# Norms issued a stage ahead of their transposes in a hybrid decoder layer, last sums stored from ScalarE's queue, the second block's operands loaded ahead

## The chip, the cores and the metric

The kernel runs on one core of one Trainium2 chip. The core has TensorE (PE; its weight loads are shown apart as PEld), VectorE (DVE), ScalarE (ACT), GpSimd (POOL) and SyncE (SP, which here only issues DMAs). The metric is the device time of one execution in microseconds (us), lower is better. A profile is one execution seen by the hardware profiler; its span runs from the first to the last recorded instruction.

## What is computed

One layer of a hybrid decoder on 2048 tokens of width 1024, in float32:

```python
h = rmsnorm(x, g_mix); z = h @ w_in
y_a = rwkv7_mix(...) @ w_out_a;  y_b = multiscale_pool_mix(...) @ w_out_b
merged = gates[:, :, 0] * y_a + gates[:, :, 1] * y_b
x = x + merged @ w_o
h = rmsnorm(x, g_mlp)
x = x + jnp.square(jax.nn.relu(h @ w_ff1)) @ w_ff2          # 1024 -> 4096 -> 1024
h = rmsnorm(x, g_ple)
x = x + jax.nn.sigmoid(h @ w_ple_gate) * (p @ w_ple_proj)   # gate stage
return rmsnorm(x, g_final)
```

The change touches the end of `merged @ w_o`, the MLP and the gate stage.

## The kernel before

**Matrix products.** A float32 operand is split into two parts of a type that PE takes at full rate (`split`, L1101 to 1103): ACT casts the value (L1102), DVE or POOL subtracts the cast from it (L1103). A product of two split operands is three matmuls (`mm3`, through L133). Transposes are PE instructions too (`tr`, L137).

**Order.** PE executes in the order of the program. A scheduler orders the instructions of the other engines and of SP's DMA queue by its own timeline; on the chip each engine and each queue then runs strictly in that order, waiting where it has to.

**Norm.** `norm_tile` (L173) norms 128 tokens: ACT squares and sums the row (L160, tile `junk`), DVE makes the reciprocal root of it in ten small steps (L165, L149 to 155) and multiplies the tile (L173, 128x1024).

**Stage B of the token mixer** ends with `merged @ w_o`, `stage_B(NB - 1, None)`, a generator that hands over control some 87 times. Between its steps the heads of the MLP's block 0 run (`heads0`, `head`, L1105 to 1162): for each of four token groups j, load and norm two tiles of the stage's result, 16 transposes in two halves, and the sums and differences of the quarters (`A11`, `S1`, ...) for a product scheme with 7 instead of 8 block products. In `head` norm and transposes of one group follow one another, and one step is made at every third hand-over from n = 34. Behind the loop `combine` (L1167 on) loads and prepares the first weights of the MLP.

**MLP layer 1** runs 16 pairs of hidden slices for each of two blocks of 1024 tokens (`pair`), 7 products of 12 matmuls each, and stores the activations to memory. During block 0, from pair 2, two steps of `heads1` per pair make block 1's operands, again norm and transposes in a row, and store them to `hD`. In the last pair of block 0, `load_home` fetches each operand of block 1 once its slot has been used last.

**MLP layer 2** has 56 products (2 blocks, 4 chunks, 7 products), each 48 matmuls on four pairs of operand tiles. The tiles come from a ring: 6 of the pool `hx` and 12 of `f3`. For each pair ACT casts both, POOL subtracts for the one and DVE for the other, and POOL forms the weights' sums. In the last chunk of each block DVE adds up the results and SP stores them to `x2D` (L1393): 16 stores a block.

**Gate stage**, 16 tiles j of 128 tokens: `norm_in` (load from `x2D`, norm, 8 transposes into `rc`, split into `ht`), `embed` (tile of p, 2 transposes, split), `gate(j, n)` for the two halves n of the columns (24 matmuls each), `put(j, n)` (6 matmuls with `wp` into `rp`, tanh on ACT, DVE products, final norm and store). In iteration j of the loop the norm and transposes of tile j+3 and the embedding of j+1 come ahead of gate j; the buffers for `xt` are two. The gate weights `wg` come in four loads of two rows of k each, both column halves together.

## Time and profile before

| what | us |
|---|---|
| median of 3 runs | 3462.11 (3458.47 to 3463.95) |
| the profiled execution: its own time | 3463.73 |
| its span, first to last instruction | 3461.9 |
| token mixer, to the last product of `merged @ w_o` | about 0 to 1721 |
| MLP layer 1 | 1721.75 to about 2434 |
| MLP layer 2 | about 2434 to 3055 |
| gate stage | 3055 to 3461.9 |
| granted clock of PE, mean over the span | 0.949 |

How to read the rows that follow: an engine's timeline gives start, duration, engine, line, operation and tiles (out <- in), how many instructions the row sums up, and in brackets how long the engine was idle ahead of it and what ended that. The granted clock is the share of its full rate that PE was allowed; after idle time it is below 1.00 for a while.

### The profile page before, as it was taken

Reading aid. Unit: us, or ns where it says so; the run is one execution under the profiler, and the core shown is the slowest. Engines: PE = TensorE matmul, PEld = TensorE weight load, DVE = VectorE, ACT = ScalarE, POOL = GpSimd, SP = SyncE. Lnnn points to the kernel's source line nnn. Section 1 sums busy time; section 2 is a strip of 40 time slices with the busy share of each in tenths; the row PEclk is TensorE's granted clock in tenths of the full one; section 3 lists DMA queues with packets and bytes.
Section 4 is the critical chain, followed back from the end, with each engine's and each line's share of the span. In section 5 each row is a group of like instructions: output and inputs, shape, how many; then the busy total and the mean of one; then the engine's idle time right before and its main releaser. Section 6 shows DMA issues by size and latency. Waiting matters only on the chain. (4 is left out here: it accounts for less than half of the span.)

```text
span 3461.9 us, 44299 instructions
## 1 busy us (share of the span) xinstructions
PE 3093.9 (89%) x14409; PEld 2515.9 (73%) x14409; DVE 2473.3 (71%) x5424; ACT 1336.5 (39%) x2774; POOL 1669.3 (48%) x1657
## 2 busy tenths in 40 slices
PE   7999999999999988798788898999899999957678
PEld 6777777777878777676576676888788878845556
DVE  4489888888888889852776867766676976764444
ACT  4446544554455444321322223222444354421111
POOL 4655444434334445311254547565998898820000
PEclk9999999999999999899898999999999999978888
DMA  7866767666666667677444555444644645341211
GB/s 242 248 212 209 237 196 235 226 225 193 209 215 206 196 220 255 210 274 260 151 161 150 180 178 199 144 152 147 246 147 145 216 161 183 110 165 66 72 61 50
DMA packets 421923, 636.41 MB, mean 184 GB/s; under 512 B 174206, under 2 KB 286396, under 8 KB 390460
## 3 DMA queue, kind: packets, MB, share of 16 engines
q1 hardware_dynamic: 421692, 633.59, 55.4%
q8 instruction: 114, 1.87, 0.2%
q14 instruction: 117, 0.96, 0.1%
HBM read 439.49 MB, written 193.99 MB: 183 GB/s over the span
## 5 line engine op out<-in xcount | busy, mean ns | idle before, releaser
L133 PE MATMUL d<-big,wf 128*128 128x512 f32 (+1 forms) x3288 | 849.1, 406 | 14.6 <-DVE wf L244 7.0
L133 PEld LDWEIGHTS d<-big,wf 128*128 128x128 f32 x3288 | 610.2, 193 | 152.6 <-DVE wf L244 9.3
L1103 DVE TENSOR_TENSOR op<-w,op 128x512 fp32r<-128x512 f32 x224 | 300.6, 1361 | 129.6 <-ACT op L1102 127.6
L1103 POOL TENSOR_TENSOR op<-hr,op 128x512 fp32r<-128x512 f32 x224 | 340.3, 1537 | 68.0 <-ACT op L1102 67.9
L133 PE MATMUL d<-op 128*128 128x512 f32 x1344 | 313.9, 392 | 8.9 <-ACT op L1102 5.1
L133 PEld LDWEIGHTS d<-op 128*128 128x128 f32 x1344 | 253.0, 189 | 65.3 <-ACT op L1102 5.5
L1102 ACT CAST op<-hr 128x512 fp32r<-128x512 f32 x224 | 139.1, 621 | 308.9 <-PE rc L133 91.0
L872 DVE TENSOR_TENSOR Xtmp<-Xt,At 128x16 f32<-128x16 f32 (+15 forms) x512 | 243.0, 475 | 9.3
L1103 POOL TENSOR_TENSOR op<-wr,op 128x512 fp32r<-128x512 f32 x96 | 139.3, 1460 | 212.5 <-ACT op L1102 212.5
L133 PE MATMUL d<-yx,wf 128*128 128x512 f32 x768 | 208.5, 418 | 21.2 <-ACT yx L390 13.8
L133 PE MATMUL d<-wf,big 128*128 128x512 f32 x768 | 202.3, 417 | 25.6 <-DVE t2k L611 17.3
L133 PE MATMUL d<-wg,ht 128*128 128x512 f32 x768 | 199.1, 417 | 0.0
L133 PEld LDWEIGHTS d<-wf,big 128*128 128x128 f32 x768 | 148.2, 198 | 64.2 <-DVE t2k L611 20.5
L1250 POOL TENSOR_TENSOR t<-t,t 128x512 f32<-128x512 f32 x128 | 188.8, 1485 | 10.9 <-issue 5.6
L133 PEld LDWEIGHTS d<-yx,wf 128*128 128x128 f32 x768 | 148.2, 199 | 58.4 <-ACT yx L390 15.5
L133 PEld LDWEIGHTS d<-wg,ht 128*128 128x128 f32 x768 | 153.9, 203 | 36.8
L1102 ACT CAST op<-wr 128x512 fp32r<-128x512 f32 x192 | 110.2, 618 | 178.8 <-DMA wr<-in_w_ff_dram 111.1
L133 PE MATMUL rp<-op 128*128 128x512 f32 x672 | 172.4, 391 | 2.8 <-POOL op L1103 2.8
L133 PE MATMUL rc<-op 128*128 128x512 f32 x672 | 171.1, 390 | 0.6 <-DVE accP L1384 0.6
L244 POOL TENSOR_TENSOR wf<-wr,wf 128x640 fp32r<-128x640 f32 (+2 forms) x69 | 120.3, 1745 | 76.4 <-ACT wf L241 71.8
L1102 ACT CAST op<-w 128x512 fp32r<-128x512 f32 x224 | 138.1, 617 | 45.6 <-POOL w L1344 20.6
L875 DVE TENSOR_REDUCE Xt<-Xtmp 128x8 f32<-128x16 f32 (+15 forms) x512 | 147.4, 288 | 9.2
(317 smaller groups left out, 6419.4 us busy)
## 6 DMA issues: line engine op xcount, KB each, us to landing
wf<-wc SPq DMA_DIRECT2D x131, 1024.0 KB, 5.3
wc<-wf SPq DMA_DIRECT2D x50, 1024.0 KB, 6.4
wr<-in_w_ff_dram SPq DMA_DIRECT2D x64, 512.0 KB, 4.9
w<-in_w_ff_dram SPq DMA_DIRECT2D x64, 512.0 KB, 6.2
wr<-in_w_in_dram SPq DMA_DIRECT2D x51, 512.0 KB, 4.5
zD<-t2k SPq DMA_DIRECT2D x96, 256.0 KB, 3.9
zs<-zD SPq DMA_DIRECT2D x32, 640.0 KB, 6.3
At<-aD SPq DMA_DIRECT2D x32, 512.0 KB, 5.2
```

What stands on the lines that cost most here:

```text
L133: PE.matmul(out_, lhsT, rhs, start=start, stop=stop, **kw)
L244: eng.tensor_tensor(wf[:, 1, c], raw[:, c], hi.bitcast(F32)[:, c], ALU.subtract)
L872: DVE.tensor_tensor(tmp[:, :, :, 0:n], Xt[:, :, 0:n].unsqueeze(2).broadcast_to([P, MCOL, FS, n]), At[:, 0:n, r:n].rearrange("p s r -> p r ...
L875: DVE.tensor_reduce(Xt[:, :, r:n].unsqueeze(3), tmp[:, :, :, 0:n], AX.X, ALU.add)
L1102: ACT.copy(out=dst[0], in_=src)
L1103: eng.tensor_tensor(dst[1], src, dst[0].bitcast(F32), ALU.subtract)
L1250: eng.tensor_tensor(out_, a, b, op)
```

## The change

Six edits:

1. `head` is cut in two: `normed` (load and norm) and `head` (transposes and sums). `heads0` norms two groups ahead, at hand-overs 2 and 12; transposes follow at every fourth hand-over from 33, and `combine` is called at n = 86, inside the loop.
2. `heads1` spreads a group over three pairs: norm, first eight transposes, second eight; it starts at pair 1.
3. `load_home` only loads, `fill_home` splits; the first two loads are issued ahead of the last pair of block 0, each fill issues the load after the next.
4. The ring of MLP layer 2 has 10 instead of 12 tiles of `f3` (16 in all). The norm vector and the norms of gate tiles 0 and 1 are issued four products before the end, their transposes inside the last product; the operand tiles of `hx` hold the result.
5. The 16 stores of the last block's sums go to ACT's DMA queue.
6. The gate weights come by column halves, 4 rows of k a load. In the loop, the load and norm of tile j+3 and the transposes of tile j+2 stand behind the first half of gate j, the embedding of j+1 behind the second; `xt` has three buffers.

```diff
+        def normed(blk, j, pool, xt, junk):
             for e, x_ in enumerate(xt):
                 SP.dma_start(out=x_, in_=x1D[...])
                 norm_tile(pool, x_, gb, x_, junk)
-                yield
+            return xt
+        def head(blk, j, xt, tmp, pss):
...
         def heads0():
+            xts = [norm0(0)]
+            yield
+            xts.append(norm0(1))
+            yield
             for j in range(4):
-                yield from head(0, j, fg, load, t2k, dict(tag="t2k", bufs=5), (rps, cps))
+                hd = head(0, j, xts.pop(0), t2k, (rps, cps))
+                next(hd)
+                yield
+                next(hd)
+                yield
+                next(hd, None)
+                if j + 2 < 4:
+                    xts.append(norm0(j + 2))
+                yield
+        steps = {2, 12, *range(33, 33 + 4 * 12, 4)}
         for n, y in enumerate(stage_B(NB - 1, None)):
-            if n >= 34 and n % 3 == 0:
+            if n in steps:
                 next(hg, None)
-        for _ in hg:
-            pass
-        ops_next = combine(fg, 0, WR, t2k)
+            if n == 86:
+                ops_next = combine(fg, 0, WR, t2k)
...
+    def fill_home(nm):
+        raw = hraws.pop(nm)
         for k, eng in ((slice(0, 2), DVE), (slice(2, 4), POOL)):
             split(...)
+        n = USE.index(nm) + 2
+        if n < len(USE):
+            load_home(USE[n])
...
     def heads1():
         for j in range(4):
-            yield from head(1, j, f2, load, tmp2, dict(tag="t2", bufs=NT2), (dps, dps))
+            xt = normed(1, j, f2, [t[:, 0, :], t[:, 1, :]], dict(tag="t2", bufs=NT2))
+            yield
+            hd = head(1, j, xt, tmp2, (dps, dps))
+            next(hd)
+            yield
+            for _ in hd:
+                pass
+            yield
...
+        if blk + 1 < NBLK and pr == NPR - 1:
+            for nm in USE[0:2]:
+                load_home(nm)
-        if blk == 0 and pr >= 2:
-            next(hg, None)
+        if blk == 0 and pr >= 1:
             next(hg, None)
...
-    ring.update(pool=f3, b=12, n=0)
+    ring.update(pool=f3, b=10, n=0)
...
         for p_, (a, b) in enumerate(cur):
+            if n + 1 == len(seq) and p_ >= 2:
+                turn_in(p_ - 2, dps)
...
-                SP.dma_start(out=x2D[rows_of(blk, e, j), ns], in_=s[k])
+                (ACT if blk + 1 == NBLK else SP).dma_start(out=x2D[rows_of(blk, e, j), ns], in_=s[k])
...
+        if n + 4 == len(seq):
+            gb = gvec(g_ple[0])
+            for j in range(2):
+                norm_in(j, f3, 2)
...
     for j in range(NT):
-        if j + 3 < NT:
-            norm_in(j + 3)
-        if j + 1 < NT:
-            embed(j + 1)
-        if j + 2 < NT:
-            load_x2(j + 2)
         for n in range(2):
             wait.append((j, n, gate(j, n)))
+            if n == 0:
+                if j == 0:
+                    embed(0)
+                if j + 1 < NT:
+                    load_p(j + 1)
+                if j + 3 < NT:
+                    norm_in(j + 3, f4, 3)
+                if j + 2 < NT:
+                    turn_in(j + 2, cps)
+            else:
+                if j + 1 < NT:
+                    embed(j + 1)
+                if j + 2 < NT:
+                    load_x2(j + 2)
```

The order on the engines shows what moved. **PE in the gate loop**, before; `xt` is a normed tile, `pt` a tile of p, `wg` and `wp` the gate and projection weights (numbers tell tiles apart):

```order
L133 MATMUL rp<-wp_27584,pT 128x512 x3
L133 MATMUL rp<-wp_27590,pT 128x512 x3
L137 MATMUL rc<-ident,xt 128x128 x8
L137 MATMUL rc<-ident,pt 128x128 x2
L133 MATMUL d<-wg_27490,ht 128x512 x3
L133 MATMUL d<-wg_27496,ht 128x512 x3
```

and now, at the end of the first half of a gate:

```order
L133 MATMUL d<-wg_27553,op 128x512 x3
L137 MATMUL rc<-ident,xt 128x128 x8
L133 MATMUL rp<-wp_27621,pT 128x512 x3
L133 MATMUL rp<-wp_27624,pT 128x512 x3
L133 MATMUL d<-wg_27593,op 128x512 x3
L133 MATMUL d<-wg_27596,op 128x512 x3
```

The eight transposes moved from ahead of a gate's first half to behind it, and belong to a later tile; `op` is the tile that was called `ht`.

**PE from the last product of layer 2 to the gate stage**, before (`rp` and `rc` are the product's sums):

```order
L133 MATMUL rp<-op 128x512 x6
L133 MATMUL rc<-op 128x512 x6
L137 MATMUL rc<-ident,xt 128x128 x16
L137 MATMUL rc<-ident,pt 128x128 x2
L137 MATMUL rc<-ident,xt 128x128 x16
L137 MATMUL rc<-ident,pt 128x128 x2
L133 MATMUL d<-wg_27490,ht 128x512 x3
```

and now:

```order
L133 MATMUL rp<-op 128x512 x6
L133 MATMUL rc<-op 128x512 x6
L137 MATMUL d<-ident,xt 128x128 x8
L133 MATMUL rp<-op 128x512 x6
L133 MATMUL rc<-op 128x512 x6
L137 MATMUL d<-ident,xt 128x128 x8
L133 MATMUL rp<-op 128x512 x6
L133 MATMUL rc<-op 128x512 x6
L133 MATMUL d<-wg_27530,op 128x512 x3
```

The transposes of tiles 0 and 1 went into the last product, those of tile 2 behind the first gate half, and the first gate matmul follows the last product at once. ACT's queue has the last four stores to `x2D` ahead of the eight casts for this gate half.

**DVE in MLP layer 1**, the second norm of block 1's group 0 before; L1250 evicts a product (`d_17869` is the last of the pair ahead of the group's transposes), L1256 is the squared ReLU:

```order
L1250 TENSOR_TENSOR t2_17752<-t2_17752,d_17869 128x512
L1256 SCALAR_TENSOR_TENSOR t2_17783<-t2_17783 128x512
L155 SCALAR_TENSOR_TENSOR rs_yn_17721<-rs_qn_17723,rs_yn_17721 128x1
L1256 SCALAR_TENSOR_TENSOR t2_17752<-t2_17752 128x512
L1103 TENSOR_TENSOR op_17985<-wr_17974,op_17985 128x512
L173 SCALAR_TENSOR_TENSOR hr_17692<-hr_17692,rs_yn_17721,gb_16403 128x1024
```

and now, for group 0 (L1276 is the old L1250; `rp_17718` is the last product ahead of the transposes):

```order
L1282 SCALAR_TENSOR_TENSOR t2_17690<-t2_17690 128x512
L1103 TENSOR_TENSOR op_17671<-wr_17649,op_17671 128x512
L173 SCALAR_TENSOR_TENSOR hr_17541<-hr_17541,rs_yn_17570,gb_16403 128x1024
L1103 TENSOR_TENSOR op_17813<-wr_17809,op_17813 128x512
L1276 TENSOR_TENSOR t2_17632<-t2_17632,d_17695 128x512
L1276 TENSOR_TENSOR t2_17601<-t2_17601,rp_17718 128x512
```

and for group 1 (`d_18255` is the last product ahead of its transposes):

```order
L1276 TENSOR_TENSOR t2_18138<-t2_18138,d_18255 128x512
L1282 SCALAR_TENSOR_TENSOR t2_18169<-t2_18169 128x512
L154 TENSOR_TENSOR rs_qn_18109<-rs_qn_18109,rs_hn_18108 128x1
L1103 TENSOR_TENSOR op_18357<-wr_18346,op_18357 128x512
L1282 SCALAR_TENSOR_TENSOR t2_18138<-t2_18138 128x512
L155 SCALAR_TENSOR_TENSOR rs_yn_18107<-rs_qn_18109,rs_yn_18107 128x1
L173 SCALAR_TENSOR_TENSOR hr_18078<-hr_18078,rs_yn_18107,gb_16403 128x1024
```

For group 0 the second L173 moved ahead of the pair's last evictions; for group 1 it stands behind them, as group 0's did.

More of the change, by code (lines that the diff above doesn't have):

```diff
@@ L1103, in split @@
             eng.tensor_tensor(dst[1], src, dst[0].bitcast(F32), ALU.subtract)
-        def head(blk, j, pool, load, tmp, junk, pss):
-            xt = load()
+        def normed(blk, j, pool, xt, junk):
             for e, x_ in enumerate(xt):
@@ L1190, in combine, with norm0 @@
             return ops
+        hraw = {nm: hr() for nm in ("A22", "S4")}
+        def norm0(j):
+            return normed(0, j, fg, [fg.tile([P, D], F32, name="xt", tag="wr", bufs=WR) for _ in range(2)],
+                          dict(tag="t2k", bufs=5))
         def heads0():
[L1193 to L1194 removed]
+            xts = [norm0(0)]
+            yield
+            xts.append(norm0(1))
+            yield
             for j in range(4):
[L1196 to L1198 removed]
+                hd = head(0, j, xts.pop(0), t2k, (rps, cps))
[7 more added lines that the diff above has]
+                yield
         hg = heads0()
+        steps = {2, 12, *range(33, 33 + 4 * 12, 4)}
         for n, y in enumerate(stage_B(NB - 1, None)):
[L1201 removed]
+            if n in steps:
                 next(hg, None)
[L1203 to L1205 removed]
+            if n == 86:
+                ops_next = combine(fg, 0, WR, t2k)
         for nm in ("A22", "S4"):
@@ L1245, in prod @@
         if last:
-            load_home(FIRST[nm])
+            fill_home(FIRST[nm])
         return ps
@@ L1283, in heads1 @@
     def heads1():
-        def load():
+        for j in range(4):
             t = hr((P, 2, D))
-            return [t[:, 0, :], t[:, 1, :]]
-        for j in range(4):
-            yield from head(1, j, f2, load, tmp2, dict(tag="t2", bufs=NT2), (dps, dps))
+            xt = normed(1, j, f2, [t[:, 0, :], t[:, 1, :]], dict(tag="t2", bufs=NT2))
[6 more added lines that the diff above has]
+            yield
     hg = heads1()
@@ L1355, in rows_of, with norm_in, turn_in @@
         return slice(blk * TC + e * 512 + j * P, blk * TC + e * 512 + (j + 1) * P)
+    hts, xts = {}, {}
+    def norm_in(j, pool, bufs):
+        xts[j] = xt = pool.tile([P, D], F32, name="xt", tag="xt", bufs=bufs)
+        SP.dma_start(out=xt, in_=x2D[j * P:(j + 1) * P, :])
+        norm_tile(pool, xt, gb, xt, dict(tag="tj", bufs=1))
+    def turn_in(j, ps):
+        xt = xts.pop(j)
+        hts[j] = ht = [hx.tile([P, 2, 512], FR, name="op", tag="op", bufs=ring["a"]).rearrange(
+            "p s (k t) -> p (s k) t", t=P) for _ in range(2)]
+        for h in range(2):
+            pt = ps()
+            for k in range(4):
+                tr(pt[:, k * P:(k + 1) * P], xt[:, (4 * h + k) * P:(4 * h + k + 1) * P], ident)
+            ks = slice(4 * h, 4 * h + 4)
+            split((ht[0][:, ks, :], ht[1][:, ks, :]), pt.rearrange("p (k t) -> p k t", t=P), DVE)
     seq = [(blk, c, nm) for blk in range(NBLK) for c in range(NCH) for nm in ORDER]
@@ L1372, in hybrid_kernel @@
             b_, c_, nm_ = seq[n + 1]
+            if n + 3 >= len(seq):
+                ring["n"] = 0 if n + 3 == len(seq) else ring["a"]
             nxt = operands(b_, c_, nm_, w2[b_ * NCH + c_])
@@ L1419, in hybrid_kernel, with weights, load_p @@
     wpv = w_ple_proj[0].rearrange("(k p) c -> p k c", p=P)
-    wgs, wps, hts, pts, xs, fss = {}, {}, {}, {}, {}, {}
+    wgs, wps, pts, xs, fss = {}, {}, {}, {}, {}
     NT = T // P
-    def weights(view, res, pool, q, nm):
+    def weights(view, res, pool, n, ks, nm):
         raw = hr()
-        SP.dma_start(out=raw.rearrange("p (k n) c -> p k (n c)", n=2), in_=view[:, 2 * q:2 * q + 2, :])
-        for i in range(4):
-            k, n = divmod(i, 2)
-            t = pool.tile([P, 2, 512], FR, name=f"{nm}{2 * q + k}{n}")
-            split((t[:, 0, :], t[:, 1, :]), raw[:, i, :], (DVE, POOL)[n])
-            res[2 * q + k, n] = t
-    def norm_in(j):
-        xt = f4.tile([P, D], F32, name="xt", tag="xt", bufs=2)
-        SP.dma_start(out=xt, in_=x2D[j * P:(j + 1) * P, :])
-        norm_tile(f4, xt, gb, xt, dict(tag="t4", bufs=4))
-        hts[j] = ht = f4.tile([P, 2, 8, P], FR, name="ht", tag="ht", bufs=4)
-        for h in range(2):
-            pt = cps()
-            for k in range(4):
-                tr(pt[:, k * P:(k + 1) * P], xt[:, (4 * h + k) * P:(4 * h + k + 1) * P], ident)
-            ks = slice(4 * h, 4 * h + 4)
-            split((ht[:, 0, ks, :], ht[:, 1, ks, :]), pt.rearrange("p (k t) -> p k t", t=P), DVE)
+        SP.dma_start(out=raw[:, 0:len(ks), :], in_=view[:, ks[0]:ks[-1] + 1, (lo, hi)[n]])
+        for i, k in enumerate(ks):
+            t = pool.tile([P, 2, 512], FR, name=f"{nm}{k}{n}")
+            split((t[:, 0, :], t[:, 1, :]), raw[:, i, :], (DVE, POOL)[i % 2])
+            res[k, n] = t
+    praw = {}
+    def load_p(j):
+        praw[j] = f4.tile([P, 256], F32, name="pt", tag="pt", bufs=2)
+        SP.dma_start(out=praw[j], in_=pv[j * P:(j + 1) * P, :])
     def embed(j):
-        pt = f4.tile([P, 256], F32, name="pt", tag="pt", bufs=2)
-        SP.dma_start(out=pt, in_=pv[j * P:(j + 1) * P, :])
+        pt = praw.pop(j)
         ps = cps()
```

30 lines of the change are left out of this document (14 added, 16 removed).

## The prediction

> **What bounds the kernel now.** I read the page's top first: busy time by engine, and the 40 slices.
>
> ```profile
> PE 3093.9 (89%) x14409; PEld 2515.9 (73%) x14409; DVE 2473.3 (71%) x5424; ACT 1336.5 (39%) x2774; POOL 1669.3 (48%) x1657
> ...
> PE   7999999999999988798788898999899999957678
> ...
> PEclk9999999999999999899898999999999999978888
> ```
>
> TensorE (PE) is the engine nearest to full, and its lowest stretch that this change can touch is the last five slices, the gate stage. Its granted clock falls there too. The sums below therefore count PE's idle time in the stages that the change touches, and the slow matmuls behind each idle time. Next came the windows (busy time and count of PE, PEld, DVE, ACT and POOL, then clock, DMA share and GB/s) for the head stage of block 1 in MLP layer 1, the loop over gate tiles 1 to 12, for that loop without transposes, and for the middle of MLP layer 2.
>
> ```profile
> 1722.00:2102.00 380.00, 336.27 (x1444) 271.93 (x1444) 281.74 (x424) 101.81 (x174) 204.54 (x135) 0.93 0.52 170
> 3112.42:3389.94 277.52, 192.94 (x770) 152.47 (x771) 122.73 (x396) 54.91 (x121) 0.00 (x0) 0.84 0.20 66
> 3408.65:3422.85 14.20, 14.20 (x63) 11.42 (x62) 6.38 (x20) 2.79 (x7) 0.00 (x0) 1.00 0.20 74
> 2500.00:2700.00 200.00, 200.00 (x881) 164.93 (x880) 145.40 (x152) 84.94 (x152) 183.45 (x123) 1.00 0.42 148
> ```
>
> In MLP layer 2 PE is never idle: nothing can be won there, only lost. In the gate loop PE works 193 of 277.5 us, and no other engine is full: DVE has 122.7/11 = 11.2 us per tile, ACT 5.0, and the DMA queues 66 GB/s. What ends PE's waits is seen in PE's timeline (start, duration, work; in brackets the idle time ahead and who ended it).
>
> ```profile
> 3112.42 1.94 PE L137 MATMUL rc<-ident,xt 128*128 128x128 f32 x8 [7.09 <-DVE xt L173]
> 3114.91 0.69 PE L137 MATMUL rc<-ident,pt 128*128 128x128 f32 x2 [0.55 <-DVE ht L1103]
> 3115.25 6.58 PE L133 MATMUL d<-wg,ht 128*128 128x512 f32 x24
> ...
> 3123.05 5.77 PE L133 MATMUL d<-wg,ht 128*128 128x512 f32 x24
> ...
> 3389.94 1.94 PE L137 MATMUL rc<-ident,xt 128*128 128x128 f32 x8 [7.14 <-DVE xt L173]
> ...
> 3408.65 0.38 PE L137 MATMUL rc<-ident,pt 128*128 128x128 f32 x2
> ...
> 3422.85 0.38 PE L137 MATMUL rc<-ident,pt 128*128 128x128 f32 x2
> ...
> 3437.05 5.76 PE L133 MATMUL d<-wg,ht 128*128 128x512 f32 x24
> ```
>
> Each tile waits some 7.1 us for the last step of its norm (L173), and works slowly afterwards (6.58 us against 5.77). A tile takes (3389.94 - 3112.42)/11 = **25.23 us**; the last tiles, which have no transposes ahead of them, take 3422.85 - 3408.65 = **14.20 us**, with PE full at clock 1.00.
>
> **1. Gate stage.** First the loop. Afterwards the eight transposes of tile j+2 stand behind the first half of gate j, and their norm was issued a stage earlier. What eight transposes cost on a warm PE stands in MLP layer 1, whose other rows serve further down:
>
> ```profile
> 1816.99 2.82 PE L137 MATMUL d<-ident,hr 128*128 128x128 f32 x12 [9.79 <-DVE hr L173]
> ...
> 1872.81 1.09 PE L137 MATMUL d<-ident,hr 128*128 128x128 f32 x4 [9.53 <-DVE hr L173]
> 1873.55 4.99 PE L133 MATMUL d<-hA,op 128*128 128x512 f32 x12
> 1878.38 2.96 PE L133 MATMUL d<-hS,op 128*128 128x512 f32 x12
> ...
> 1895.12 1.04 PE L137 MATMUL d<-ident,hr 128*128 128x128 f32 x8
> ...
> 1937.66 1.53 PE L137 MATMUL d<-ident,hr 128*128 128x128 f32 x12 [1.70 <-DVE hr L173]
> ```
>
> A tile then takes 14.20 + 1.04 = 15.24 us, 10.0 us less: 7.14 of wait, 0.55 of the wait for the split, 2.3 of slow clock. Is the norm in time? Its chain, and what else the start of the stage rests on:
>
> ```profile
> 3108.68 0.15 DVE L165 TENSOR_SCALAR nmsn<-nss 128x1 f32<-128x1 f32 x1 [1.83 <-ACT junk L160]
> ...
> 3110.99 1.28 DVE L173 SCALAR_TENSOR_TENSOR xt<-xt,rs_yn,gb 128x1024 f32<-128x1024 f32 x1
> ...
> xt<-x2D SPq DMA_DIRECT2D x6, 512.0 KB, 8.4
> ...
> 3062.50 1.06 ACT L160 ACTIVATE junk<-xt 128x1024 bf16<-128x1024 f32 x1 [18.06 <-DMA xt<-x2D]
> ...
> 3069.90 2.18 ACT L1102 CAST wg<-hr 128x512 fp32r<-128x512 f32 x4
> ...
> 3044.18 14.39 SPq L1393 DMA_DIRECT2D x2D<-accP x12
> 3058.62 0.95 SPq L1436 DMA_DIRECT2D xt<-x2D x2
> ...
> 3053.73 1.52 PE L133 MATMUL rc<-op 128*128 128x512 f32 x6
> ...
> 3092.09 11.86 PE L133 MATMUL d<-wg,ht 128*128 128x512 f32 x48
> ```
>
> From a free buffer to a normed tile it takes 8.4 (load), 1.06 (squares) and 3.6 on DVE (from 3108.68 to 3110.99 + 1.28): 13 us. With three buffers a load starts when the tile three back has been transposed, three periods (45 us) ahead of its own transposes. On ACT the squares of tile j+5 stand right behind the casts of tile j+2, so ACT may sit some 8 us in that wait; its 5.0 us of work per tile still fit into 15.24, and the tanh behind it is needed only a half-tile later. DVE's 11.2 us fit too. I take **no wait in the loop**; the bound is 3 us per tile, if ACT's wait and the final norm's stores meet (13 x 3 = +39).
>
> The start. Let T = 3053.73 + 1.52 = 3055.25, the end of the last product. Before, the first gate matmul came at 3092.09, T+36.8, since SP, blocked for 14.39 us in waits of the last stores, issued the loads of the first tiles only at 3058.62, and load, norm and transposes followed one another. Afterwards tiles 0 and 1 are normed before the end and transposed within the last product (16 transposes at 1.04 for eight, which move T by +2.1). But ACT's queue now holds the last four stores ahead of the casts of the gate weights: the last store was issued at 3044.18 + 14.39, T+3.3. Eight casts at 2.18/4 take 4.4 us, T+7.7; subtractions trail by a microsecond or two; gate(0, first half) ends near T+13 on a slow clock. Tile 2 is normed (1.06 + 3.6) and transposed by about T+15. On SP the load of tile 5 waits for that, and ahead of the last half-load of the second weight half stands that load; on ACT the squares of tile 5 (load 8.4 us: T+24) stand ahead of the last four casts (2.18) and their subtractions: T+28. So gate(0, second half) ends at **T+30**. Bounds: T+25, if only casts and matmuls count, and T+40, if the weight load queues behind 2 MB of other loads.
>
> From there: 0.4 + 1.55 for the two transposes and the projection, 13 tiles x 15.24 = 198.1, one of 14.20, and the last tile with its tail, 3461.9 - 3437.05 = 24.85. The sum is 2.1 + 30 + 1.9 + 198.1 + 14.2 + 24.85 = 271.2 us after T, against 3461.9 - 3055.25 = 406.65. **-135** (-140 to -86).
>
> A rule that speaks against a part of this stands in the Trainium skill, "DMA: Bandwidth & Descriptors", section "Issuing engines are not separate DMA queues": transfers issued from several engines run on the same 16 DMA engines, and a second issuer saves only the sequencer's time, which it calls small. By that rule the moved stores bring nothing. The 14.39 us of SP above are not issue time, though, but an in-order queue held by waits for DVE. By the rule alone the start would be T+30 + 3.4 (the issue of 3058.62 instead of T), and the total 3.4 us higher.
>
> **2. Norms of block 1 inside MLP layer 1.** The groups by line for both MLP head stages (busy, mean ns, then idle ahead and who ended it); the first of them is from the window 1722 to 2102, the others from 1607 to 1722. Ahead of them stand three rows of PE's timeline.
>
> ```profile
> 1616.11 23.30 PE L133 MATMUL d<-yx,wf 128*128 128x512 f32 x87 [8.08 <-ACT yx L390]
> ...
> 1650.78 2.34 PE L133 MATMUL d<-wf,big 128*128 128x512 f32 x9
> ...
> 1708.70 4.19 PE L133 MATMUL d<-wf,big 128*128 128x512 f32 x9
> ...
> L137 PE MATMUL d<-ident,hr 128*128 128x128 f32 x64 | 12.1, 342 | 39.1 <-DVE hr L173 39.1
> ...
> L133 PE MATMUL d<-wf,big 128*128 128x512 f32 x192 | 53.7, 438 | 7.9 <-DVE t2k L636 6.1 <-DVE t2k L611 1.8
> ...
> L137 PE MATMUL rp<-ident,xt 128*128 128x128 f32 x32 | 5.8, 312 | 6.0 <-DVE rs_qn L153 5.3 <-DVE xt L173 0.7
> L137 PE MATMUL rc<-ident,xt 128*128 128x128 f32 x32 | 5.6, 304 | 4.7 <-DVE xt L173 4.7
> ```
>
> 39.1 us of waits, and about 5 of slow clock behind them (4.99 against 2.96 for twelve matmuls, 2.82 against 1.53 for twelve transposes): 44. The change norms one pair (seven products like the 2.96 above) ahead of the first transposes, so a second half no longer waits. But DVE runs in order, and there the second L173 of token groups 1 and 3 still stands behind the last evictions of the pair, as that of group 0 did before (9.79); for groups 0 and 2 it stands ahead of the last ones, as that of group 2 did (1.70). Two at about 8 and two at 1.7 leave 19.4, and 3 of slow clock. **-22** (-10 if every group still waits 8; -35 if none waits over 2).
>
> **3. Norms of block 0 beside the last token-mixer block.** 6.0 + 4.7 = 10.7 us of waits for norms go, and some 3 of slow clock (1.85 of it in nine matmuls, 4.19 against 2.34). The 7.9 us that wait for evictions (L636, L611) stay: the loads they use stand on SP behind the weight loads of the next pair, which now wait for transposes of group 2. The two early norms stand on DVE and ACT ahead of the 8.08 us in which PE waits, in the first row above, and are short enough for it. **-12** (-5 to -20).
>
> **4. Block 1's operands loaded ahead (load_home).** The two loads stood on SP ahead of their pair already before the change, by the scheduler's own choice, and the seven stand in the same order now. **0** (-5 to +5).
>
> **5. Ring of 16 instead of 18 in MLP layer 2.** A product of 48 matmuls takes 200/881 x 48 = 10.9 us and uses four pairs of operand tiles, one every 2.73 us. A ring one pair smaller shortens the lead of POOL (183.45 of 200 us busy) by 2.73 us. Where it falls behind already, at the change of blocks, PE waits now:
>
> ```profile
> 2778.10 2.56 PE L133 MATMUL d<-op 128*128 128x512 f32 x10 [1.50 <-POOL op L1103]
> 2782.27 1.21 PE L133 MATMUL rp<-op 128*128 128x512 f32 x4 [1.16 <-POOL op L1103]
> ```
>
> That becomes one pair longer: **+3** (0 to +15, if it comes back at every third chunk). The two norms hoisted into layer 2 (2 x 1.06 on ACT, 2 x 3.6 on DVE) lie beside full PE work, with ACT at 85 of 200 us and DVE at 145; without that cover they would cost up to 9.
>
> **Sum:** -135 - 22 - 12 + 0 + 3 = -166. The profiled run took 3463.73 us (1.83 around its span, which I leave as it is), so 3297.7; the median of the runs shown is 1.6 us lower, and I predict **3296**.
>
> **Rivals.**
> - *The loop still waits.* For it: ACT's queue has the squares of a tile whose load was just issued ahead of the tanh. Against: the half-tile of slack. 3 us x 13 = +39: 3335.
> - *The head stages give nothing*, because evictions and norms share DVE and one wait takes the other's place (282 of 380 us of DVE are busy in the window row above; the 7.9 us for evictions are such waits). +34: 3330.
> - *More goes than I count*: no wait over 2 us in any head, gate(0) done at T+25, and the waits at the block change gone: -5 - 13 - 8 - 3 = 3267.
> - *Slower: the ring of 16 starves PE throughout layer 2.* POOL is 92% busy; if a slot came free too late for its in-order queue at every pair, each of the 56 products would grow. The change turns into a loss from 166/56 = 3.0 us per product, 13.9 instead of 10.9; at 4 us it would be 3296 + 56 x 4 = 3520. Against: POOL's work per product is 183.45/200 x 10.9 = 10.0 us, so even with no lead it keeps up; a partial form, 1 us per product, gives 3352.
>
> **How the numbers follow.** Forecast 0.72 (own range 3275 to 3318), loop waits 0.09, heads give nothing 0.08, more than counted 0.06, starving 0.05 (of which 0.02 from the point where it loses). The range 3272 to 3336 leaves out the starved cases, half of the better one and the outer part of the others, under 0.2. Within 0.2% (7 us, about what a measurement of this kernel can tell from no change) lies nearly nothing: faster 0.97, same 0.01, slower 0.02.
>
> **What would show it.** Right: in the gate loop a period near 15.2 us, clock 1.00, and no idle row of PE ended by L173; the first gate matmul about 10 us after the last product; two of the four first transposes in layer 1 still behind a wait of 6 to 10 us; PE rows of layer 2 without idle time except at the block change. Wrong: a gate period over 16 us with rows ended by ACT; waits on `op` spread over layer 2; L636 waits longer than 8 us in all.

## The result and the profile after

The changed kernel takes 3303.95 us (median of 4 runs, 3301.6 to 3314.85), the one before 3460.83 us on the same chip: a ratio of **0.9552 (0.953 to 0.9575)**, 157 us less. The prediction was 3296, with a range of 3272 to 3336. The profiled execution took 3303.20 us, with a span of 3301.4.

The page's top of the changed kernel, busy time by engine and the slices:

```profile
PE 3054.8 (93%) x14409; PEld 2492.0 (75%) x14409; DVE 2455.9 (74%) x5424; ACT 1336.2 (40%) x2774; POOL 1653.8 (50%) x1657
...
PE   7999989999999998788989889899989998999998
...
PEclk9999999999999999899999999899999999999999
```

The hollow at the end of the PE row is gone, and with it the low clock there. Where the 160.5 us between the two profiled spans went is seen by cutting both spans at the same instructions of PE:

| stretch, cut at PE's rows | before | after | difference | predicted |
|---|---|---|---|---|
| start to the last 87 `yx,wf` matmuls | 1616.1 | 1611.2 | -5.0 | 0 |
| from there to the first matmul of layer 1 | 105.6 | 88.9 | -16.7 | -12 |
| layer 1 | 704.3 | 689.6 | -14.7 | -22 |
| layer 2 | 629.2 | 647.4 | **+18.2** | +5.1 |
| end of the last product to the end | 406.6 | 264.4 | **-142.3** | -137.1 |

(The 2.1 us of the transposes that went into the last product are put to layer 2 here; the prediction had them in its -135. In layer 1, 4.4 us belong to the stage ahead: waits of its first pair, 2.12 and 2.28 before and none after. Layer 2 begins at 2426.0 in the kernel before, 8 us earlier than the table of times before the change has it.) The first row is no effect: the mixer's code is the same, and that cut lies between 1609.0 and 1621.5 in the profiles of this study.

The gate stage is the prediction's picture. PE's timeline after (start, duration, work, idle time ahead):

```profile
3035.49 1.54 PE L133 MATMUL rc<-op 128*128 128x512 f32 x6
3041.69 8.68 PE L133 MATMUL d<-wg,op 128*128 128x512 f32 x24 [4.66 <-ACT wg L1102]
...
3058.95 7.28 PE L133 MATMUL d<-wg,op 128*128 128x512 f32 x16 [6.33 <-ACT wg L1102]
3066.43 2.43 PE L133 MATMUL d<-wg,op 128*128 128x512 f32 x8 [0.20 <-POOL wg L1103]
...
3075.80 1.03 PE L137 MATMUL rc<-ident,xt 128*128 128x128 f32 x8
3076.59 1.64 PE L133 MATMUL rp<-wp,pT 128*128 128x512 f32 x6
3078.06 5.61 PE L133 MATMUL d<-wg,op 128*128 128x512 f32 x24
...
3253.55 1.03 PE L137 MATMUL rc<-ident,xt 128*128 128x128 f32 x8
```

With T = 3037.03, the end of the last product, the first gate matmul comes at T+4.7 (predicted: about 10 us after T), the first half ends at T+13.3 (predicted: near T+13) and the second at T+31.8 (predicted: T+30). The 6.33 us ahead of the second half end when ACT casts its weights, and ACT itself had waited for their load:

```profile
3058.28 2.18 ACT L1102 CAST wg<-hr 128x512 fp32r<-128x512 f32 x4 [2.33 <-DMA hr<-in_w_ple_gate_dram]
```

A tile takes (3253.55 - 3075.80)/12 = 14.81 us without any idle row and at a granted clock of 1.00; 15.24 were predicted, and 25.23 were taken before. Transposes on a warm PE cost less than their row: the next row starts 0.79 us behind, not 1.04.

What the prediction had not seen is in layer 2, at the change of blocks:

```profile
2733.38 8.71 PE L133 MATMUL d<-op 128*128 128x512 f32 x37 [1.41 <-ACT accP L1440]
2744.37 2.79 PE L133 MATMUL d<-op 128*128 128x512 f32 x11 [2.29 <-DVE op L1103]
2759.43 2.90 PE L133 MATMUL rp<-op 128*128 128x512 f32 x6 [12.27 <-DVE accP L1442]
```

PE waits 16 us there, against 3.3 before, 12.27 of them for DVE to empty a sum. What DVE did in that time is the norm of the two gate tiles, which the scheduler had hoisted to this place (rows of DVE and of POOL):

```profile
2745.09 0.14 DVE L151 TENSOR_SCALAR rs_hn<-nmsn 128x1 f32<-128x1 f32 x1
2745.21 0.15 DVE L150 TENSOR_SCALAR rs_yn<-rs_yn 128x1 int32<-128x1 int32 x1
2745.39 0.69 DVE L153 TENSOR_TENSOR rs_qn<-rs_yn 128x1 f32<-128x1 f32 x1
2746.12 1.21 DVE L154 TENSOR_TENSOR rs_qn<-rs_qn,rs_hn 128x1 f32<-128x1 f32 x1
2747.37 1.19 DVE L155 SCALAR_TENSOR_TENSOR rs_yn<-rs_qn,rs_yn 128x1 f32<-128x1 f32 x1
...
2756.44 2.25 DVE L173 SCALAR_TENSOR_TENSOR xt<-xt,rs_yn,gb 128x1024 f32<-128x1024 f32 x1
2758.61 0.67 DVE L1442 TENSOR_TENSOR accP<-accP,rp 128x512 f32<-128x512 f32 x1
```

```profile
2749.72 7.89 POOL L1103 TENSOR_TENSOR op<-hr,op 128x512 fp32r<-128x512 f32 x6
```

The reciprocal root of a norm is 13 such steps on 128x1 numbers, not the ten named further up: four that read one tensor, and three rounds of L153 to L155, which read two. A step of these rounds took up to 1.2 us here, and 0.16 in the gate loop, where POOL has nothing to do. The steps follow one another at about 1.22 us, POOL's six instructions at 7.89/6 = 1.3: the two engines take turns. The steps with one tensor operand (L151, L150) stay at 0.14 to 0.15 us between them.

### The profile page after: what moved, and what is told of

Read it like the earlier page. It is cut to its first block, busy times and chain, and to the rows that moved or that the text cites. A ratio compares the mean times of both kernels' runs of the same rounds, so it can differ in the third digit from the quotient of the medians.

```text
span 3301.4 us, 44294 instructions
## 1 busy us (share of the span) xinstructions
PE 3054.8 (93%) x14409; PEld 2492.0 (75%) x14409; DVE 2455.9 (74%) x5424; ACT 1336.2 (40%) x2774; POOL 1653.8 (50%) x1657
## 5 line engine op out<-in xcount | busy, mean ns | idle before, releaser
L1103 DVE TENSOR_TENSOR op<-w,op 128x512 fp32r<-128x512 f32 x224 | 287.4, 1295 | 139.2 <-ACT op L1102 137.8
L1103 POOL TENSOR_TENSOR op<-hr,op 128x512 fp32r<-128x512 f32 x224 | 331.2, 1494 | 95.5 <-ACT op L1102 95.5
L133 PE MATMUL d<-wg,op 128*128 128x512 f32 x768 | 187.0, 399 | 11.3 <-ACT wg L1102 11.0
L1276 POOL TENSOR_TENSOR t<-t,t 128x512 f32<-128x512 f32 x128 | 189.4, 1490 | 9.8 <-issue 5.6
L133 PE MATMUL rp<-op 128*128 128x512 f32 x672 | 173.5, 393 | 13.9 <-DVE accP L1442 12.3
L133 PEld LDWEIGHTS d<-wg,op 128*128 128x128 f32 x768 | 147.1, 192 | 46.4 <-ACT wg L1102 11.6
L133 PEld LDWEIGHTS rp<-op 128*128 128x128 f32 x672 | 126.9, 190 | 42.0 <-issue 12.7
```

What stands on the lines that cost most here:

```text
L133: PE.matmul(out_, lhsT, rhs, start=start, stop=stop, **kw)
L1103: eng.tensor_tensor(dst[1], src, dst[0].bitcast(F32), ALU.subtract)
L1276: eng.tensor_tensor(out_, a, b, op)
```

## The experiments

Each kernel is the kernel before or the changed one with a small edit. Times are medians; the ratio is to the kernel before on the same chip; the changed kernel's own is 0.9552.

| kernel | us | ratio (95%) |
|---|---|---|
| before + ring of 16 (ring10) | 3465.16 | 1.001 (1.0 to 1.0019) |
| changed, late norms (late) | 3295.60 | 0.9523 (0.9503 to 0.9544) |
| changed, short chain (chain) | 3278.00 | 0.9466 (0.9448 to 0.9483) |
| changed, stores on SP (spstore) | 3316.88 | 0.9577 (0.9558 to 0.9596) |
| changed, norm and transposes in one stage (samestage) | 3315.40 | 0.958 (0.9566 to 0.9595) |
| changed, old heads of block 1 (oldheads1) | 3318.85 | 0.9586 (0.9568 to 0.9603) |
| changed, old load_home (oldhome) | 3306.32 | 0.9561 (0.9544 to 0.9578) |
| before + own scrap buffer (ownjunk) | 3360.19 | 0.9703 (0.9687 to 0.9719) |
| changed, shared scrap buffers (sharedjunk) | 3309.42 | 0.9556 (0.954 to 0.9572) |
| changed, old heads of block 0 (oldheads0) | 3330.95 | 0.9617 (0.9601 to 0.9632) |
| short chain, late norms, ring of 18 (chain_late12) | **3267.90** | 0.9445 (0.943 to 0.9461) |
| the same, four stores on SP (mixed) | 3273.57 | 0.946 (0.9439 to 0.948) |

### Layer 2: the ring or the hoisted norms?

ring10, the kernel before with the smaller ring alone:

```diff
-    ring.update(pool=f3, b=12, n=0)
+    ring.update(pool=f3, b=10, n=0)
```

> The kernel before with one number changed: the ring of layer 2 has 16 operand tiles instead of 18. Layer 2 took 18 us longer in the changed kernel than before (2389.63 to 3037.03 against 2426.02 to 3055.25). If the smaller ring were the cause: 12 to 18 us slower than the kernel before, with TensorE waits for operand tiles spread over layer 2. If the cause is the two norms that the scheduler hoisted to the block change: within 4 us of the kernel before.

Measured: 0.1% slower, some 3 us, with an interval that reaches from 0 to 0.19%; layer 2 takes 630.0 us from its first matmul to the end of its last product, 0.8 more than before. The ring is not the cause. The prediction's +3 lies within the interval, but the wait that was to grow did not: PE's idle rows at the change of blocks sum up to 3.4 us here and 3.3 before.

late, the changed kernel with the two norms kept away from the block change:

```diff
-        xts[j] = xt = pool.tile([P, D], F32, name="xt", tag="xt", bufs=bufs)
+        xts[j] = xt = (src or pool).tile([P, D], F32, name="xt", tag=tag, bufs=bufs)
...
-                norm_in(j, f3, 2)
+                norm_in(j, f3, 12, g3, "w2")
```

> The changed kernel, but the tiles of the two hoisted norms take slots of the weight tiles of layer 2, which come free only ahead of the last chunk, so the norms cannot run at the block change. If the norms there are the cause of the 12.27 us wait: it vanishes, and the kernel is 10 to 16 us faster than the changed one (near 3290). If the smaller ring is the cause: the wait moves but stays, within 3 us of the changed kernel (near 3303).

Measured: 3295.6, 8 us less than the changed kernel by the medians (10 to 16 were expected) and 0.29% by the ratios, whose intervals overlap a little. The trace decides. PE's rows at the block change:

```profile
2743.50 3.06 PE L133 MATMUL d<-op 128*128 128x512 f32 x12 [0.35 <-POOL op L1103]
2748.13 2.56 PE L133 MATMUL d<-op 128*128 128x512 f32 x10 [1.56 <-POOL op L1103]
2751.86 1.19 PE L133 MATMUL rp<-op 128*128 128x512 f32 x4 [0.72 <-POOL op L1103]
```

The 12.27 are gone, what is left are the small waits that the kernel before had too, and layer 2 takes 632.4 us instead of 647.4 (it takes 646.5 to 648.2 in the other kernels here that have the norms at the block change with the old steps). The norms now run from 2925.9 to 2940.4, where POOL has gaps of 1.5 to 3.3 us, and no row of PE waits. So **the 15 us are the two norms at a place where DVE and POOL are both busy.** The other stretches of this profile add up to 7 us more than in the changed kernel, 1.7 of them at the start of the gate stage, where the first gate matmul waits 5.93 us instead of 4.66; the rest lies ahead of the edit.

### What makes a norm so dear there?

chain, the changed kernel with other instructions for the same arithmetic. A step no longer reads two tensors; the second and third number come as per-partition scalars, and three instructions become two:

```diff
         for _ in range(iters):
+            if n == 1:
+                DVE.tensor_scalar(q, y, y[:, 0:1], h[:, 0:1], op0=ALU.mult, op1=ALU.mult)
+                DVE.tensor_scalar(y, q, 1.5, y[:, 0:1], op0=ALU.add, op1=ALU.mult)
+                continue
             DVE.tensor_tensor(q, y, y, ALU.mult)
```

> The changed kernel, but each step of the reciprocal root (three small DVE instructions, of which all read two tensors) is two instructions that read one tensor and take the others as per-partition scalars. Theory: a small DVE instruction with two tensor operands waits for GpSimd's running instruction (1.0 to 1.2 us beside GpSimd, 0.16 alone), one with a single tensor does not (0.15 in both places). Then the six instructions take 0.15 to 0.2 us each everywhere, the wait of 12.27 us at the block change and those of 10.19 and 10.13 us in layer 1 shrink to a few us, and the kernel is 15 to 30 us faster than the changed one (3275 to 3290). Rival: any small DVE instruction is held up there, by queueing and not by its operands; then they still take about 1 us each, a third fewer of them, and 3 to 8 us are won.

Measured: 3278.0, 26 us less than the changed kernel, as the theory of the operands had it; the rival's 3 to 8 are out. By the profiles layer 2 is 14.4 us shorter (633.0) and layer 1 16.5 us (673.1). The groups of DVE by line around the block change, with the two norms in it, first in the changed kernel (2725 to 2760; busy, mean ns, idle ahead):

```profile
L155 DVE SCALAR_TENSOR_TENSOR rs_yn<-rs_qn,rs_yn 128x1 f32<-128x1 f32 x6 | 7.3, 1218 | 0.2
L154 DVE TENSOR_TENSOR rs_qn<-rs_qn,rs_hn 128x1 f32<-128x1 f32 x6 | 6.2, 1026 | 0.2
L153 DVE TENSOR_TENSOR rs_qn<-rs_yn 128x1 f32<-128x1 f32 x6 | 6.0, 1001 | 0.2
...
L149 DVE TENSOR_SCALAR rs_yn<-nmsn 128x1 int32<-128x1 int32 x2 | 0.3, 154 | 0.1
```

and with the short chain (2700 to 2760):

```profile
L154 DVE TENSOR_SCALAR rs_qn<-rs_yn,rs_hn 128x1 f32<-128x1 f32 x6 | 1.6, 273 | 0.2
L155 DVE TENSOR_SCALAR rs_yn<-rs_qn,rs_yn 128x1 f32<-128x1 f32 x6 | 1.3, 210 | 0.1
L149 DVE TENSOR_SCALAR rs_yn<-nmsn 128x1 int32<-128x1 int32 x2 | 0.3, 154 | 0.1
```

The new steps take 273 and 210 ns beside POOL, and 268 and 208 ns in the gate stage, where POOL is idle: no wait for POOL is left in them, and the price of the scalar operands, more than the 0.15 to 0.2 us expected, is the same in both places. So a DVE instruction waits here for POOL by its operands, not by its size or its place in the queue. The Trainium skill says it on the page "SBUF — State Buffer", section "Who interferes with whom": the ports that DVE and GpSimd share are an exclusive lock; a DVE instruction with two inputs in SBUF contends for them with a GpSimd instruction that reads SBUF, while one with at most one such input, outside the modes that use two ports, does not. The trace agrees, with 1.0 to 1.2 us against 0.16 for the one and 0.27 against 0.27 for the other.

The same shows in layer 1, in PE's waits ahead of the transposes of block 1, 28.8 us in all in the changed kernel and 14.7 with the short chain (rows of the changed kernel first):

```profile
1824.56 0.66 PE L137 MATMUL d<-ident,hr 128*128 128x128 f32 x4 [1.97 <-DVE hr L173]
1835.41 1.09 PE L137 MATMUL d<-ident,hr 128*128 128x128 f32 x4 [10.19 <-DVE hr L173]
...
1972.55 1.11 PE L137 MATMUL d<-ident,hr 128*128 128x128 f32 x4 [10.13 <-DVE hr L173]
```

```profile
1828.92 1.09 PE L137 MATMUL d<-ident,hr 128*128 128x128 f32 x4 [6.17 <-DVE hr L177]
...
1958.91 1.11 PE L137 MATMUL d<-ident,hr 128*128 128x128 f32 x4 [6.44 <-DVE hr L177]
```

Not all of it goes: the last step of the norm (128x1024, two tensors) still takes its turn with POOL (2.30 us at 1826.48, against 1.28 beside an idle POOL), and it still stands behind the pair's last evictions.

### The gate loop: what fills it?

samestage, the changed kernel with norm and transposes of a tile in a row again, ahead of a gate:

```diff
     for j in range(NT):
+        if j and j + 2 < NT:
+            norm_in(j + 2, f4, 3)
+            turn_in(j + 2, cps)
         for n in range(2):
...
-                if j + 3 < NT:
-                    norm_in(j + 3, f4, 3)
-                if j + 2 < NT:
-                    turn_in(j + 2, cps)
+                if j == 0:
+                    turn_in(2, cps)
```

> The changed kernel, but in the gate loop the load, norm and transposes of tile j+2 stand together ahead of gate j, as the old order had them (there for tile j+3). If issuing the norm a stage ahead is what fills TensorE in the loop: the wait for the last norm step comes back, a tile takes 22 to 25 us instead of 14.81, and the kernel takes 90 to 130 us more than the changed one (3390 to 3435). If the gain came from the weights by column halves, the third buffer for tiles or the stores, and the loop would be full anyway: within 10 us of the changed kernel.

A miss, and the most useful one: 3315.4, only some 11 us more than the changed kernel. PE's rows in its loop show a wait of 0.4 to 0.5 us a tile, not 7:

```profile
3106.45 1.06 PE L137 MATMUL rc<-ident,xt 128*128 128x128 f32 x8 [0.47 <-DVE xt L173]
...
3121.97 1.06 PE L137 MATMUL rc<-ident,xt 128*128 128x128 f32 x8 [0.47 <-DVE xt L173]
```

So the order of the calls, which the change is named after, is not needed for the loop. What else differs from the kernel before? The loads of `xt` were never late there: SP issued them more than a whole tile ahead (at 3114.39 for the squares at 3158.48, with two buffers). Late were the squares on ACT, which stood behind the output stage of the tile before. ACT's timeline before:

```profile
3157.85 0.63 ACT L1481 ACTIVATE junk<-x 128x512 bf16<-128x512 f32 x1 [5.92 <-DVE x L1477]
3158.39 0.19 ACT L1481 ACTIVATION_READ_ACCUMULATOR junk<-x 128x1 f32 x1
3158.48 1.04 ACT L160 ACTIVATE junk<-xt 128x1024 bf16<-128x1024 f32 x1
```

The squares' result is scrap (only the sum is used), and its buffer was one of the four `t4` that the tanh results and the scrap of the output stage use as well. The change gives it a buffer of its own, `tj`, a detail inside the new `norm_in` that the list of edits and the prediction had passed over. ownjunk, the kernel before with that alone:

```diff
-        norm_tile(f4, xt, gb, xt, dict(tag="t4", bufs=4))
+        norm_tile(f4, xt, gb, xt, dict(tag="tj", bufs=1))
```

> The kernel before with one change: the squares of a gate tile's norm write their scrap result into a buffer of its own (one), as in the changed kernel, and no longer into the four shared with the tanh results and scrap tiles of the output stage. Theory, formed after the run with norm and transposes in one stage (only 11 us slower): the order of the calls hardly matters; the four shared buffers, handed out in program order, held each norm's squares behind the output stage of the tile before, and so TensorE waited 7.1 us a tile. Then most of the loop's gain appears here, with everything else as before: the wait ahead of the transposes falls below 2 us and 80 to 115 us are won (3347 to 3382). Rival (the order of calls, or the third tile buffer): under 20 us won.

Measured: 3360.19, 104 us less than the kernel before on its chip, with two buffers for `xt` and the old order of calls. PE's rows in its loop:

```profile
3117.74 1.06 PE L137 MATMUL rc<-ident,xt 128*128 128x128 f32 x8 [0.44 <-DVE xt L173]
3119.77 0.44 PE L137 MATMUL rc<-ident,pt 128*128 128x128 f32 x2 [0.96 <-DVE ht L1103]
...
3134.68 1.06 PE L137 MATMUL rc<-ident,xt 128*128 128x128 f32 x8 [0.49 <-DVE xt L173]
```

A tile takes 3134.68 - 3117.74 = 16.94 us instead of 25.23. **One line about a scrap buffer, added to the kernel before, is worth two thirds of what the whole change won.** The waits that remain, 0.4 to 0.5 us for the norm and 0.96 for the split of the tile, do not occur in the new order.

sharedjunk, the counterpart: the changed kernel with the scrap back in the shared four:

```diff
-        norm_tile(pool, xt, gb, xt, dict(tag="tj", bufs=1))
+        norm_tile(pool, xt, gb, xt, dict(tag="tj", bufs=1) if j < 2 else dict(tag="t4", bufs=4))
```

> The changed kernel, but from tile 2 on the norm's scrap result goes into the four shared buffers again, as before the change. Theory of the shared buffers: the squares of a tile stand behind the output stage again, and a wait for the norm comes back in the loop; since the transposes now stand half a gate later, a part of it stays hidden: a tile takes 16 to 20 us instead of 14.81, 15 to 65 us slower than the changed kernel (3320 to 3370). Rival (order of calls): within 5 us.

A miss again: 3309.42, a ratio of 0.9556 against 0.9552, no difference. A tile takes 14.81 us as in the changed kernel, with no idle row. With the new order the scheduler puts the squares one tile earlier even in shared buffers (the squares at 3116.93 are for the transposes at 3134.90), and that is early enough. So the own buffer is enough to free most of the loop, and so is the new order with its third `xt` buffer (a tile takes 15.5 us with the old order of norm and transposes, 14.81 with the shared buffers, 16.94 in the kernel before with the own buffer), and undoing one of them shows next to nothing: only ownjunk, an addition to the kernel before, found what the wait was made of. What the third `xt` buffer does alone, and the new order without it, wasn't tried; ownjunk shows that neither is needed.

### The stores on ACT's queue

spstore, the changed kernel with the 16 stores on SP:

```diff
-                (ACT if blk + 1 == NBLK else SP).dma_start(out=x2D[...], in_=s[k])
+                SP.dma_start(out=x2D[...], in_=s[k])
```

> The changed kernel with the last block's 16 stores on SyncE's queue again. By the rule that a second issuing engine only saves issue time: within 4 us of the changed kernel. If SyncE's queue held in waits was what delayed the gate stage's loads: the loads of tile 2 and of the second half of the gate weights go out 3 to 10 us later, and the kernel is 3 to 10 us slower (3306 to 3314); the first gate matmul may come earlier, since ScalarE's casts no longer stand behind the stores.

Measured: 3316.88 (3310.54 to 3317.96); the ratios' intervals (0.9577 and 0.9552) overlap, and part of the difference of the medians lies ahead of the edit: its token mixer came 9.4 us later. From the trace: tile 1's first gate matmul comes 3085.07 - 3046.69 = 38.4 us after the last product, in the changed kernel 3070.33 - 3037.03 = 33.3. SP's queue in spstore, then in the changed kernel:

```profile
3033.27 19.88 SPq L1451 DMA_DIRECT2D x2D<-accP x12
3053.20 0.45 SPq L1498 DMA_DIRECT2D pt<-in_p_dram  x1
3053.69 0.45 SPq L1395 DMA_DIRECT2D xt<-x2D  x1
```

```profile
3029.86 0.33 SPq L1498 DMA_DIRECT2D pt<-in_p_dram  x1
3031.12 0.33 SPq L1395 DMA_DIRECT2D xt<-x2D  x1
```

So the moved stores are worth about 5 us: from the end of the last product to the end spstore takes 269.5 us, and the four kernels here that share the changed gate stage (the changed one, oldheads0, oldheads1, oldhome) 264.2 to 264.6. The load of tile 2 goes out 5.9 us ahead of the end of the last product instead of 7.0 behind it. With the casts freed of the stores, one gate matmul follows the last product at once (3046.53), but the next waits 6.52 us for the subtraction of the weights, which DVE does behind the last sums; against 4.66 us of wait in the changed kernel nothing is won there. By the Trainium skill, "DMA: Bandwidth & Descriptors", section "Issuing engines are not separate DMA queues", a second issuing engine saves only issue time, and next to nothing should have been lost. The trace differs, since the 19.88 us of SP's queue were mostly waits for DVE, with loads queued behind them.

mixed, chain_late12 with the last four stores back on SP:

```diff
-                (ACT if blk + 1 == NBLK else SP).dma_start(out=x2D[...], in_=s[k])
+                (ACT if blk + 1 == NBLK and nm != "P3" else SP).dma_start(out=x2D[...], in_=s[k])
```

> The version with the shorter chain, late norms and 18 operand tiles (chain_late12), with the last four stores, those of the last product, back on SyncE's queue and the other twelve on ScalarE's. If ScalarE's casts of the gate weights wait only for the stores queued ahead of them: the wait of 4.68 us ahead of the first gate matmul falls below 2 us, and 3 to 6 us are won (3262 to 3265). If the loads behind those four stores on SyncE come later by as much: the wait ahead of the second gate half grows by what the first lost, and nothing is won (within 3 us of 3267.9).

Neither came: it is 5.7 us slower than chain_late12 by the medians, with intervals that overlap, and by the profiles 3.8 us slower behind the last product (268.3 against 264.5). As in spstore one gate matmul comes at once and the next waits 6.53 us for the subtraction on DVE (4.68 for the casts in chain_late12), the loads go out behind the four stores (`xt` 7.0 us after the last product), and the transposes of tile 1's embedding come 35.7 us after the last product instead of 31.9. By the traces all 16 on ACT is the best of the three.

### The other parts, undone one by one

oldheads0, the changed kernel with the old order at the end of the token mixer:

```diff
-            if n in steps:
-                next(hg, None)
-            if n == 86:
-                ops_next = combine(fg, 0, WR, t2k)
+            if n >= 34 and n % 3 == 0:
+                next(hg, None)
+        for _ in hg:
+            pass
+        ops_next = combine(fg, 0, WR, t2k)
```

> The changed kernel with the norms and transposes of block 0 at the end of the token mixer as before (every third step from 34, the weights combined behind the loop). The stage and the first pair behind it lost some 17 to 21 us by the traces of the two kernels; the prediction had 12. If the edit did that: 15 to 22 us slower than the changed kernel (3319 to 3326). If the difference came from elsewhere (the end of the token mixer varies by some us between runs): 8 to 13 us slower.

Measured: 0.9617 against 0.9552, 22 us of 3461; 27 by the medians, at and above the upper end of what was expected. By the profiles the stage is 16.5 us longer and layer 1 6.7. The waits are those of the kernel before (PE's groups by line, oldheads0, from its last `yx,wf` matmuls to layer 1):

```profile
L137 PE MATMUL rc<-ident,xt 128*128 128x128 f32 x32 | 5.8, 312 | 4.7 <-DVE xt L173 4.7
L137 PE MATMUL rp<-ident,xt 128*128 128x128 f32 x32 | 5.4, 294 | 6.0 <-DVE rs_qn L153 5.2 <-DVE xt L173 0.7
```

oldheads1, the changed kernel with two steps a pair from pair 2, and norm and transposes in a row:

```diff
-            xt = normed(1, j, f2, [t[:, 0, :], t[:, 1, :]], dict(tag="t2", bufs=NT2))
-            yield
...
+            for e in range(2):
+                SP.dma_start(out=xt[e], in_=x1D[...])
+                norm_tile(f2, xt[e], gb, xt[e], dict(tag="t2", bufs=NT2))
+                yield
+            yield from head(1, j, xt, tmp2, (dps, dps))
...
-        if blk == 0 and pr >= 1:
+        if blk == 0 and pr >= 2:
             next(hg, None)
+            next(hg, None)
```

> The changed kernel with the norms and transposes of block 1 in layer 1 as before (two steps a pair from pair 2, norm and transposes in a row). In the changed kernel TensorE's waits there sum up to 29 us against 39 before. Theory (the order gained about 10 us, since what holds the second norm is DVE beside GpSimd): 8 to 14 us slower than the changed kernel (3312 to 3318). Rival (the 22 us of the prediction, partly hidden by other differences): 18 to 26 us slower.

Measured: 0.9586 against 0.9552, 12 us of 3461 (15 by the medians), and layer 1 is 10.9 us longer by the profiles (700.5): the 8 to 14 that the theory gave it, not the 22 of the prediction.

oldhome, the changed kernel with each load of block 1's operands where it stood before:

```diff
         if last:
-            fill_home(FIRST[nm])
+            load_home(FIRST[nm])
+            fill_home(FIRST[nm])
...
-        if blk + 1 < NBLK and pr == NPR - 1:
-            for nm in USE[0:2]:
-                load_home(nm)
```

> The changed kernel with the loads of block 1's operands issued as before, each behind the last use of its slot in the program. The scheduler had hoisted the first two in the old kernel too. If the edit moves nothing that is waited for: within 4 us of the changed kernel, with the same waits at the block change of layer 1 (17 us of them). If it won something: 5 to 10 us slower.

Measured: 3306.32, 0.9561, no difference that can be told. The waits at the block change are the same, down to the last (5.40 us for `big` in both).

### All that helped, together

chain_late12 has the short chain, the late norms and, since the late norms need no tiles of their own in that pool, the ring of 18 again:

> The changed kernel with the shorter chain of single-tensor steps, the hoisted norms kept away from the block change of layer 2 by the slots of its weights, and 18 operand tiles again. If the causes add: the shorter chain's 26 us, of which some 9 are already those of the block change, plus 2 to 4 for the larger ring: 3272 to 3280. If the ring and the place of the norms are worth something beyond the chain: 3262 to 3272.

Measured: 3267.9 (3264.4 to 3272.09), **36 us below the changed kernel** and 193 us below the one before. Layer 2 takes 629.05 us, as before the change although it now holds 16 more transposes. It came out below the sum of the causes that the first expectation added up (3272 to 3280). Against the short chain alone the profiles have 3.9 us of it in layer 2 and 5.4 in the token mixer, whose code is the same in both, so that this part is spread.

## Why the prediction was right or wrong

- **The sum was right (predicted 3296, measured 3303.95), partly by luck, since errors cancelled.** By stretches: -137.1 predicted and -142.3 measured for the gate stage, -34 and -31.4 for the heads together, +5.1 and +18.2 for layer 2, and 5 us of the token mixer's own spread. Within the heads two errors of 10 us cancelled as well.
- **Gate loop: number right, reason incomplete.** The method, two rows of the kernel's own loop with and without the wait (25.23 and 14.20 plus transposes), gave 15.24, and 14.81 were measured. But the prediction put the whole gain to the norm's being issued a stage earlier, and its chain of reasons ("with three buffers a load starts ...") looked at the loads, which were never late. ownjunk shows that the shared scrap buffer had made the wait; samestage and sharedjunk show that the own buffer alone, or the new order with its third tile buffer, removes nearly all of it. The rival of a loop that still waits did not come.
- **Start of the gate stage: the time right, the path in part.** The second half ended at T+31.8 (predicted T+30), and the order on SP and ACT was as said. The first matmul came at T+4.7 instead of about T+10, for it waits for the first cast behind the stores and not for all eight. The wait ahead of the second half was put to the squares of a tile just loaded; it ended with the weights' own load (ACT idle for 2.33 us), and the last half-load, too, landed 1.4 us after those squares were done.
- **Norms of block 1: direction right, size wrong, -22 predicted and about -12 measured.** Two groups at about 2 and two at about 10 came where 1.7 and 8 were expected, but groups 1 and 3 waited twice (1.97 and 10.19; 2.13 and 10.13), so that 28.8 us were left instead of 19.4. What the prediction missed is why a norm ends so late beside POOL.
- **Norms of block 0: -12 predicted and about -22 measured.** The waits for norms went as said (10.7 us to nothing), the waits for evictions did not shrink (7.9 became 10.5). With 10.4 us for L636 one of the prediction's own signs of being wrong came up; why they grew is open. The rest is what the prediction left standing: the waits ahead of and in the first pair of layer 1 (2.48, 2.12 and 2.28) vanished too, and the slow clock behind them. oldheads0 has waits there again; that they hang on the weights' being combined inside the loop is likely, but that edit was not undone by itself.
- **load_home: right (0).** **The ring: +3 predicted; 0 to 6.6 us by the runs, 0.8 in layer 2**, without the longer wait that was its reason. The sentence that PE is never idle in layer 2 holds for its window (2500 to 2700): ahead of 2490 PE's idle rows sum up to 9 us before the change and 10.6 after.
- **The step that failed** is the sentence behind the ring's term: "The two norms hoisted into layer 2 (2 x 1.06 on ACT, 2 x 3.6 on DVE) lie beside full PE work ...; without that cover they would cost up to 9." The cover was counted in busy shares over 200 us; the norms landed at the change of blocks, where DVE has the sums of the old block to finish. And the 3.6 us came from a stretch with an idle POOL; beside a busy POOL they were 11.9 and 13.9 (2731.85 to 2743.71 and 2744.84 to 2758.69, with one other instruction of 0.68 in each). They cost 15 us. The trace of before could have warned: the same small steps had means of 239 to 383 ns in layer 1 against 160 in the gate stage.

## What to carry to other kernels

Before a wait is put down to the order of work, list every buffer that the late instruction needs, scrap outputs too: a shared scrap tile is a dependence that no data flow shows, and here it was worth 104 us. Price an instruction from rows in which its neighbours are as busy as they will be at its new place, and look at where the scheduler puts it, not where the code does. When a change bundles edits, add single ones to the old kernel as well as taking single ones out of the new: two edits that are each enough hide one another when undone.

## What the runs showed of the hardware

- DVE steps of 128x1 with two tensor operands took 1.0 to 1.2 us beside a busy POOL and 0.16 us beside an idle one; with one tensor and per-partition scalars 0.27 and 0.21 us in both. The nine of a norm took 9.8 us on the mean ((7.3 + 6.2 + 6.0)/2), against 1.28 us for the 128x1024 multiplication that they prepare (2.25 beside POOL).
- Eight transposes on a warm PE hold the next matmuls up by 0.79 us, three quarters of their own row.
